# One core, a three-part matmul stream: longer first weight loads, a final norm by square root and reciprocal, and a store cut by tokens

## The chip, the cores and the metric

One core of a Trainium2 chip. The metric is the device time of one execution in microseconds; the number that counts is the median over runs.

## The reference

One decoder layer on x of shape (1, 256, 1024) in float32, then a final norm:

```
x = x + 0.5 * swiglu(rmsnorm(x, ffn1_norm), ...)           # D_FF = 2816
x = x + hybrid_mixer(rmsnorm(x, mix_norm), ...)            # S5 state space + attention, gated
x = x + 0.5 * swiglu(rmsnorm(x, ffn2_norm), ...)
return rmsnorm(x, final_norm)
# rmsnorm(x, g) = x * rsqrt(mean(x*x, over features) + 1e-6) * g
```

## The kernel before

x lies transposed in SBUF: 128 partitions by 8 feature tiles by 256 tokens. All weights come as one stream of units, each 128 partitions by 1024 float32 (512 KB, eight 128x128 tiles), in the order in which TensorE uses them. A unit n passes through three steps: `load(n, i)` fetches it on the SP queue into one of four staging buffers; `hi` copies it on ScalarE to a rounded 32-bit form (tile `wh`); `lo` subtracts that from the original on VectorE (tile `wl`). TensorE then makes three matmuls for each weight tile (L188 to L190): high weight by high x, high weight by low x, low weight by high x. x is split into `xh` and `xl` in the same way by `split_x`. A norm's factor is not applied to x ahead of a matmul but to the matmul's result.

The first stage is written out by hand (L872 to L895). Seven dummy matmuls (`warm_up`) run while the first data comes. Then the SP queue issues, in this order, x tile 0 with the gains, the first two quarters of unit 0, x tile 1, the second half of unit 0, x tiles 2 and 3, the halves of unit 1, x tiles 4 and 5, the halves of unit 2, x tiles 6 and 7, the halves of unit 3, and the identity. For each x tile k in turn, ScalarE and VectorE do the work of L888 to L894: split x tile k, split the piece or pieces of weights that belong to it, square x tile k for the norm. Each engine works in the order of the program. The first four outputs of the first feed-forward are computed together, so x tile k needs four weight tiles, half a unit: unit 0's first half for k = 0, its second half for k = 1, unit 1's first half for k = 2, and so on. From unit 4 on, units are loaded whole, each when a staging buffer comes free (`load_to`).

The second feed-forward ends with eight outputs m of its down projection. After each, `after_ffn2` squares x tile m and scales it by the final norm's gain. Then `norm(diag=False, ...)` sums the squares by matmuls into two columns (one for each half of the tokens, tile `nps`), and VectorE works out the inverse root on them with an integer trick and two polynomial steps (L245 to L253). Meanwhile TensorE transposes x back to tokens by features into four PSUM tiles `turned[i][h]` (token half i, feature half h). For each feature half h, ScalarE scales token half 0 and VectorE token half 1 into one tile, and the SP queue stores it with rows of 512 elements.

Of the kernel before, what the change touches and what calls it, by code (L numbers as in the profile page):

```python
# [10 lines left out]
F32 = mybir.dt.float32  # L11
F32R = mybir.dt.float32r
I32 = mybir.dt.int32
AF = mybir.ActivationFunctionType
ALU = mybir.AluOpType
# [4 lines left out]
D = 1024  # L20
# [8 lines left out]
UT = 8  # L29
# [7 lines left out]
RMS_EPS = 1e-6  # L37
# [24 lines left out]
def hybrid_layer(ctx: ExitStack, tc: tile.TileContext, xT, wst, consts, bc, out):  # L62
    nc = tc.nc
    V, S, G, PE = nc.vector, nc.scalar, nc.gpsimd, nc.tensor
    NU = wst.shape[0]

    cp = ctx.enter_context(tc.tile_pool(name="cp", bufs=1))
# [9 lines left out]
    def tt(out, a, b, op=ALU.mult, eng=None):  # L77
        (eng or V).tensor_tensor(out=out, in0=a, in1=b, op=op)  # L78

    def ts(out, a, s1, op0, s2=None, op1=None, eng=None):  # L80
        if op1 is None:
            (eng or V).tensor_scalar(out=out, in0=a, scalar1=s1, scalar2=None, op0=op0)
        else:
            (eng or V).tensor_scalar(out=out, in0=a, scalar1=s1, scalar2=s2, op0=op0, op1=op1)

    def stt(out, a, s, b, op0, op1):
        V.scalar_tensor_tensor(out=out, in0=a, scalar=s, in1=b, op0=op0, op1=op1)

    def act(out, a, func=AF.Copy, **kw):
        S.activation(out=out, in_=a, func=func, **kw)  # L90
# [11 lines left out]
    ones = cp.tile([128, 128], F32, name="ones")  # L102
    V.memset(ones, 1.0)
    warm = cp.tile([128, 1], F32, name="warm")
    act(warm, ones[:, 0:1], AF.Silu)
    halfpi = cp.tile([128, 1], F32, name="halfpi")
    V.memset(halfpi, math.pi / 2)
    inv = cp.tile([128, T], F32, name="inv")
    inv_tm = cp.tile([128, 2], F32, name="inv_tm")
    nrm = cp.tile([128, 2, 2], F32, name="nrm")  # L110
# [8 lines left out]
    staged, split = {}, {}  # L119
    state = {"load": 0, "hi": 0, "lo": 0, "at": -1, "hold": (3, 5)}  # L120
    LA = RB - 1

    def cuts(n):
        return [0, 256, 512, 1024] if n == 0 else [0, 512, 1024] if n <= 3 else [0, 1024]

    def load(n, i):
        if i == 0:
            staged[n] = stg.tile([128, UT * 128], F32, name="stage", tag="stage")
        c = slice(*cuts(n)[i:i + 2])
        nc.sync.dma_start(out=staged[n][:, c], in_=wst[n, :, c])  # L130

    def hi(n, i):
# [11 lines left out]

    def load_to(u):
        while state["load"] <= min(u, NU - 1):
            load(state["load"], 0)
            state["load"] += 1

    def split_hi(u):  # L150
        while state["hi"] <= min(u, NU - 1):
            load_to(state["hi"])
            hi(state["hi"], 0)
            state["hi"] += 1
# [11 lines left out]
    def ahead(u):  # L166
        split_hi(u + LA)
        split_lo(u + LA - 1)
        load_to(u + LA + 2)
        while deferred:  # L170
            deferred.pop(0)()
        if u in hooks:
            hooks.pop(u)()
# [47 lines left out]
    def square(k, first):  # L221
        add_squares()
        dst = acc if first else ev.tile([128, T], F32, name="sq", tag="sq")
        act(dst, x[:, k, :], AF.Square)
        if not first:
            squares.append(dst)

    def gram(t, y, v):
        for i in range(2):
            c = slice(i, i + 1)  # L230
            stt(t[:, c], y[:, c], y[:, c], v[:, c], ALU.mult, ALU.mult)

    def norm(pool=ps_a, tag="at", diag=True, between=None):
        ps = [pool.tile([128, 1], F32, name="nps", tag=tag) for _ in range(2)]
        terms = [acc] + squares
        squares.clear()
        for n, a in enumerate(terms):
            if between and n == len(terms) - 1:
                between()
            for i in range(2):  # L240
                for o in (0, 64):
                    PE.matmul(ps[i][o:o + 64, :], a[:, i * 128 + o:i * 128 + o + 64], ones[:, 0:1],
                              start=n == 0, stop=n == len(terms) - 1)
        v, t, y = nrm[:, 0, :], nrm[:, 1, :], inv_tm
        for i in range(2):  # L245
            ts(v[:, i:i + 1], ps[i], 1.0 / D, ALU.mult, RMS_EPS, ALU.add)
        ts(y.bitcast(I32), v.bitcast(I32), -0.5, ALU.mult, RSQRT_MAGIC, ALU.add)
        gram(t, y, v)
        stt(y, t, RSQRT_B, y, ALU.subtract, ALU.mult)
        gram(t, y, v)  # L250
        ts(v, t, -0.375 * RSQRT_A ** 5, ALU.mult, 1.25 * RSQRT_A ** 3, ALU.add)
        tt(v, v, t)
        stt(y, v, 1.875 * RSQRT_A, y, ALU.subtract, ALU.mult)  # L253
        if diag:
            diags.append(ev.tile([128, 2, 128], F32, name="dg", tag="sq"))
            for i in range(2):
                ts(diags[0][:, i, :], ident, y[:, i:i + 1], ALU.mult)
# [15 lines left out]
    def ffn(pool, bg, parts, norm_at, done, g):  # L273
        kh = KF // parts
        xh, xl = xv[g]
        for f in range(parts):
# [13 lines left out]
            for j in range(kh):  # L290
                if f == 0 and j < 2:
                    if j == 0:
                        first = [psum(i) for i in range(4)]
                        for k in range(KD):
                            for i in range(4):
                                mm3(first[i], pos[0], xh[:, k, :], xl[:, k, :], k == 0, k == KD - 1)
                                pos[0] += 1
                            if k == norm_at:
                                norm(ps_s, "s5")
                                if state["at"] in state["hold"]:  # L300
                                    ahead(state["at"])
# [566 lines left out]
    def load_x(k0, k1):  # L868
        c = slice(0 if k0 == 0 else 4 * KD + k0 * T, 4 * KD + k1 * T)
        nc.sync.dma_start(out=xg[:, c], in_=xT[:, c])  # L870

    warm_up(7)  # L872
    load_x(0, 1)
    load(0, 0)
    load(0, 1)
    load_x(1, 2)
    load(0, 2)
    load_x(2, 4)
    load(1, 0)
    load(1, 1)  # L880
    load_x(4, 6)
    load(2, 0)
    load(2, 1)
    load_x(6, 8)
    load(3, 0)
    load(3, 1)
    nc.sync.dma_start(out=ident, in_=consts[:, 0:128])
    for k, parts in ((0, ((0, 0), (0, 1))), (1, ((0, 2),)), (2, ((1, 0),)), (3, ((1, 1),)), (4, ((2, 0),)), (5, ((2, 1),)),  # L888
                     (6, ((3, 0),)), (7, ((3, 1),))):
# [32 lines left out]
    with tc.tile_pool(name="f2", bufs=1) as f2:  # L922
        last = f2.tile([128, T], F32, name="last")

        def after_ffn2(m):
            if m < KD - 1:
                square(m, m == 0)
            else:
                tt(last, x[:, m, :], x[:, m, :])
                squares.append(last)  # L930
            act(x[:, m, :], x[:, m, :], scale=gn[:, 3, m:m + 1])

        ffn(f2, idle, FH2, 4, after_ffn2, 2)
        turned = [[(ps_m if i == 0 else ps_s).tile([128, 512], F32, name="tps", tag="mm" if i == 0 else "s5")
                   for h in range(2)] for i in range(2)]

        def turn_x(m):
            for i in range(2):
                o = 128 * (m % 4)
                PE.transpose(turned[i][m // 4][:, o:o + 128], x[:, m, i * 128:(i + 1) * 128], ident)  # L940

        norm(diag=False, between=lambda: [turn_x(m) for m in range(4)])
        for m in range(4, KD):
            turn_x(m)
        for h in range(2):
            o = f2.tile([128, 2, 512], F32, name=f"out{h}")
            act(o[:, 0, :], turned[0][h], scale=inv_tm[:, 0:1])
            ts(o[:, 1, :], turned[1][h], inv_tm[:, 1:2], ALU.mult)
            nc.sync.dma_start(out=out.rearrange("(i p) d -> p i d", i=2)[:, :, 512 * h:512 * h + 512], in_=o)


def _perm():
# [109 lines left out]
```

## Time and profile before

| | us |
|---|---|
| median of 3 runs | 558.54 |
| lowest, highest | 558.08, 563.71 |
| the profiled execution, device time | 557.2 |
| its span, first to last instruction | 555.3 |
| TensorE busy within the span | 544.5 |
| VectorE busy | 399.2 |
| ScalarE busy | 309.1 |

The profile is one execution, taken apart by the hardware profiler. Times are from the span's start. TensorE's matmuls are pipelined: one of 256 columns is listed with 0.28 us, though the next one starts 0.11 us later. A DMA appears twice: as an instruction of the queue that issues it, and by its landing, the time from issue until all of it has arrived.

### The profile page before, as it was taken

Reading aid. Unit: us, or ns where it says so; the run is one execution under the profiler, and the core shown is the slowest. Engines: PE = TensorE matmul, PEld = TensorE weight load, DVE = VectorE, ACT = ScalarE, POOL = GpSimd, SP = SyncE. Lnnn points to the kernel's source line nnn. Section 1 sums busy time; section 2 is a strip of 40 time slices with the busy share of each in tenths; the row PEclk is TensorE's granted clock in tenths of the full one; section 3 lists DMA queues with packets and bytes.
Section 4 is the critical chain, followed back from the end, with each engine's and each line's share of the span. In section 5 each row is a group of like instructions: output and inputs, shape, how many; then the busy total and the mean of one; then the engine's idle time right before and its main releaser. Section 6 shows DMA issues by size and latency. Waiting matters only on the chain.

```text
span 555.3 us, 11894 instructions
## 1 busy us (share of the span) xinstructions
PE 544.5 (98%) x4860; PEld 534.5 (96%) x4860; DVE 399.2 (72%) x657; ACT 309.1 (56%) x477; POOL 80.3 (14%) x150
## 2 busy tenths in 40 slices
PE   7999999999999999999999999999999999999994
PEld 7999999999999989989999999999999999999994
DVE  5886798888865776999845888786766666665643
ACT  7764546559575683336547665565555444455421
POOL 0288951957000000000000000000000000000000
PEclk9999999999999999999999999999999999999998
DMA  8876666557564445265342656564755555666502
GB/s 281 297 253 195 193 194 216 156 157 229 175 201 159 145 152 152 77 208 191 105 145 77 203 185 186 187 209 164 228 195 192 191 190 193 194 210 204 173 15 77
DMA packets 28678, 99.30 MB, mean 179 GB/s; under 512 B 3152, under 2 KB 3792, under 8 KB 28624
## 3 DMA queue, kind: packets, MB, share of 16 engines
q1 hardware_dynamic: 28624, 98.54, 55.0%
q8 instruction: 38, 0.62, 0.4%
q14 instruction: 16, 0.13, 0.1%
HBM read 97.48 MB, written 1.05 MB: 177 GB/s over the span
## 4 chain that ended last, share of the span: by engine, by line
PE 94%; DVE 3%; DMA 1%; issue 1%; SPq 0%; DVEq 0%; ACT 0%
PE mm L188 20%; PE mm L189 19%; PE mm L190 19%; PE mma L188 8%; PE mma L189 8%; PE mma L190 8%; PE bps L615 1%; PE sps L714 1%; DMA stage<-in_wst_dram 1%; PE yps L662 1%; PE ops L744 1%; DVE wl L78 1%; PE up L584 1%; PE up L586 1%; PE vp L586 1%; PE vp L585 1%
## 5 line engine op out<-in xcount | busy, mean ns | idle before, releaser
L78 DVE TENSOR_TENSOR wl<-stage,wh 128x1024 fp32r<-128x1024 f32 (+2 forms) x187 | 223.3, 1201 | 15.0 <-ACT wh L90 14.8
L90 ACT ACTIVATE wh<-stage 128x1024 fp32r<-128x1024 f32 (+2 forms) x187 | 191.5, 1030 | 56.3 <-PE mm L189 26.3
L188 PE MATMUL mm<-xhl,wh 128*128 128x256 f32 x544 | 152.1, 280 | 2.2 <-ACT wh L90 2.2
L190 PE MATMUL mm<-xhl,wl 128*128 128x256 f32 x544 | 150.9, 277 | 0.4 <-DVE wl L78 0.4
L189 PE MATMUL mm<-xhl,wh 128*128 128x256 f32 x544 | 150.4, 277 | 0.0
L188 PEld LDWEIGHTS mm<-xhl,wh 128*128 128x128 f32 x544 | 102.1, 188 | 3.5 <-ACT wh L90 2.4
L190 PEld LDWEIGHTS mm<-xhl,wl 128*128 128x128 f32 x544 | 102.2, 188 | 1.0 <-DVE wl L78 0.8
L189 PEld LDWEIGHTS mm<-xhl,wh 128*128 128x128 f32 x544 | 102.2, 188 | 0.1
L188 PE MATMUL mma<-xhl,wh 128*128 128x256 f32 x352 | 97.7, 278 | 0.0
L188 PE MATMUL mm<-ahl,wh 128*128 128x256 f32 x352 | 97.5, 277 | 0.0
L190 PE MATMUL mm<-ahl,wl 128*128 128x256 f32 x352 | 97.2, 276 | 0.0
L189 PE MATMUL mm<-ahl,wh 128*128 128x256 f32 x352 | 97.2, 276 | 0.0
L189 PE MATMUL mma<-xhl,wh 128*128 128x256 f32 x352 | 97.2, 276 | 0.0
L190 PE MATMUL mma<-xhl,wl 128*128 128x256 f32 x352 | 97.2, 276 | 0.0
L188 PEld LDWEIGHTS mm<-ahl,wh 128*128 128x128 f32 x352 | 66.1, 188 | 0.2 <-issue 0.2
L188 PEld LDWEIGHTS mma<-xhl,wh 128*128 128x128 f32 x352 | 66.1, 188 | 0.1
L189 PEld LDWEIGHTS mma<-xhl,wh 128*128 128x128 f32 x352 | 66.1, 188 | 0.1
L190 PEld LDWEIGHTS mm<-ahl,wl 128*128 128x128 f32 x352 | 66.1, 188 | 0.0
L189 PEld LDWEIGHTS mm<-ahl,wh 128*128 128x128 f32 x352 | 66.1, 188 | 0.0
L190 PEld LDWEIGHTS mma<-xhl,wl 128*128 128x128 f32 x352 | 66.0, 188 | 0.0
L90 ACT ACTIVATE gs<-gs 128x256 f32<-128x256 f32 x52 | 21.8, 418 | 54.1 <-DVE gs L78 53.8
L78 DVE TENSOR_TENSOR gs<-gs,mma 128x256 f32<-128x256 f32 x44 | 18.5, 419 | 38.5 <-PE mma L190 33.7
(214 smaller groups left out, 730.8 us busy)
## 6 DMA issues: line engine op xcount, KB each, us to landing
stage<-in_wst_dram SPq DMA_DIRECT2D x178, 512.0 KB, 3.7
stage<-in_wst_dram SPq DMA_DIRECT2D x7, 256.0 KB, 5.5
out_dram<-out SPq DMA_DIRECT2D x2, 512.0 KB, 3.2
xg<-in_xT_dram SPq DMA_DIRECT2D x3, 256.0 KB, 5.8
bct<-in_bc_dram SPq DMA_DIRECT2D x1, 512.0 KB, 5.5
cst<-in_consts_dram SPq DMA_DIRECT2D x1, 396.0 KB, 4.7
stage<-in_wst_dram SPq DMA_DIRECT2D x2, 128.0 KB, 2.5
xg<-in_xT_dram SPq DMA_DIRECT2D x1, 144.0 KB, 2.1
```

The costliest lines, as they stand in the source:

```text
L78: (eng or V).tensor_tensor(out=out, in0=a, in1=b, op=op)
L90: S.activation(out=out, in_=a, func=func, **kw)
L188: PE.matmul(ps, wh, xh, start=start, stop=False)
L189: PE.matmul(ps, wh, xl, start=False, stop=False)
L190: PE.matmul(ps, wl, xh, start=False, stop=stop)
L584: PE.matmul(acc2[i], xh[:, k, sl], wh, start=k == 0, stop=False)
L585: PE.matmul(acc2[i], xh[:, k, sl], wl, start=False, stop=False)
L586: PE.matmul(acc2[i], xl[:, k, sl], wh, start=False, stop=k == KD - 1)
L615: PE.matmul(bp[part][o, gp, :], Rt[part][:, 8 * h + gp, o], Uc[:, 8 * h + gp, :], start=True, stop=True)
L662: PE.matmul(ypf[64 * par:64 * par + 64, gg, :], l, r.rearrange("p a b -> p (a b)"), start=term == 0, stop=term == 2)
L714: PE.matmul(sps[e][:, blk, :].rearrange("p a b -> p (a b)"), q[r, i, qs], k[r, i, ks], start=part == 0, stop=part == 1)
L744: PE.matmul(op[:, i, e, :], pq[:, b, :], v[:, j, h, :], start=j == 0, stop=b != 1)
```

## The change

Three parts. The first stage's loads of weights are fewer: unit 0 comes in two halves and not in two quarters and a half, units 1, 2 and 3 each whole and not in two halves. The pieces in which `hi` and `lo` split them stay as they were. The final norm takes a square root on ScalarE (`refine`), a reciprocal on VectorE, and one Newton step in place of the integer trick and two polynomial steps; a dummy square root after the first output of the last down projection brings its function table in. The output is gathered by token halves, a full row of 1024 elements each, the first stored from the SP queue, the second from ScalarE's.

```diff
+    eps = cp.tile([128, 1], F32, name="eps")
+    V.memset(eps, RMS_EPS)
...
-    def load(n, i):
-        if i == 0:
+    def load(n, *c):
+        if n not in staged:
             staged[n] = stg.tile([128, UT * 128], F32, name="stage", tag="stage")
-        c = slice(*cuts(n)[i:i + 2])
+        c = slice(*c)
         nc.sync.dma_start(out=staged[n][:, c], in_=wst[n, :, c])
...
+    def refine(ps, v, t, y):
+        for i in range(2):
+            act(y[:, i:i + 1], ps[i], AF.Sqrt, scale=1.0 / D, bias=eps)
+        V.reciprocal(out=y, in_=y)
+        tt(t, y, y)
+        tt(t, t, v)
+        ts(t, t, -0.5, ALU.mult, 1.5, ALU.add)
+        tt(y, y, t)
...
         for i in range(2):
             ts(v[:, i:i + 1], ps[i], 1.0 / D, ALU.mult, RMS_EPS, ALU.add)
+        if not diag:
+            return refine(ps, v, t, y)
...
     load_x(0, 1)
-    load(0, 0)
-    load(0, 1)
+    load(0, 0, 512)
     load_x(1, 2)
-    load(0, 2)
+    load(0, 512, 1024)
     load_x(2, 4)
-    load(1, 0)
-    load(1, 1)
+    load(1, 0, 1024)
     load_x(4, 6)
-    load(2, 0)
-    load(2, 1)
+    load(2, 0, 1024)
     load_x(6, 8)
-    load(3, 0)
-    load(3, 1)
+    load(3, 0, 1024)
...
         def after_ffn2(m):
+            if m == 0:
+                act(warm, ones[:, 0:1], AF.Sqrt)
...
-        for h in range(2):
-            o = f2.tile([128, 2, 512], F32, name=f"out{h}")
-            act(o[:, 0, :], turned[0][h], scale=inv_tm[:, 0:1])
-            ts(o[:, 1, :], turned[1][h], inv_tm[:, 1:2], ALU.mult)
-            nc.sync.dma_start(out=out.rearrange("(i p) d -> p i d", i=2)[:, :, 512 * h:512 * h + 512], in_=o)
+        for i in range(2):
+            o = f2.tile([128, D], F32, name=f"out{i}")
+            act(o[:, 0:512], turned[i][0], scale=inv_tm[:, i:i + 1])
+            ts(o[:, 512:D], turned[i][1], inv_tm[:, i:i + 1], ALU.mult)
+            (nc.sync, S)[i].dma_start(out=out[i * 128:(i + 1) * 128, :], in_=o)
```

## Rows read from the trace of the kernel before

**Rows 1.** The page, part 1: busy time of each engine, share, instructions

```profile
PE 544.5 (98%) x4860; PEld 534.5 (96%) x4860; DVE 399.2 (72%) x657; ACT 309.1 (56%) x477; POOL 80.3 (14%) x150
```

**Rows 2.** Waits of TensorE, whole span: total us, times, longest us

```profile
PE mm L188 <- ACT wh L90: 2.2, 1, 2.2
...
PE mm L190 <- DVE wl L78: 0.4, 2, 0.2
```

**Rows 3.** The chain that ended last, first 18 us: start, us, what

```profile
3.55 5.47 DMA stage<-in_wst_dram
...
17.06 0.35 DVE acc L78
```

**Rows 4.** Timeline of ScalarE, first stage: start, us, operation, idle before and releaser

```profile
4.28 0.42 ACT L90 ACTIVATE wh<-stage 128x256 fp32r<-128x256 f32 x1 [0.30 <-DMA stage<-in_wst_dram]
...
4.91 0.49 ACT L90 ACTIVATE xhl<-xg 128x256 fp32r<-128x256 f32 x1
7.48 0.63 ACT L90 ACTIVATE wh<-stage 128x512 fp32r<-128x512 f32 x1 [2.08 <-DMA stage<-in_wst_dram]
...
9.04 0.63 ACT L90 ACTIVATE wh<-stage 128x512 fp32r<-128x512 f32 x1 [0.16 <-DMA stage<-in_wst_dram]
...
11.56 0.62 ACT L90 ACTIVATE wh<-stage 128x512 fp32r<-128x512 f32 x1
```

**Rows 5.** Timeline of the SP queue, first stage: DMA issues

```profile
1.19 0.90 SPq L130 DMA_DIRECT2D stage<-in_wst_dram  x2
...
2.60 0.43 SPq L130 DMA_DIRECT2D stage<-in_wst_dram  x1
...
3.55 0.91 SPq L130 DMA_DIRECT2D stage<-in_wst_dram  x2
```

**Rows 6.** DMA issues at 1.19, 2.60 and 4.02 us: us to landing

```profile
stage<-in_wst_dram SPq DMA_DIRECT2D x1, 128.0 KB, 2.4
...
stage<-in_wst_dram SPq DMA_DIRECT2D x1, 256.0 KB, 4.9
...
stage<-in_wst_dram SPq DMA_DIRECT2D x1, 256.0 KB, 5.7
```

**Rows 7.** Windows: length, busy by engine, granted clock, DMA share, GB/s

```profile
0.00:3.00 3.00, 1.95 (x9) 1.95 (x10) 0.17 (x2) 1.61 (x3) 0.20 (x4) 1.00 0.31 93
3.00:6.00 3.00, 2.95 (x19) 2.61 (x18) 1.82 (x4) 1.92 (x5) 0.00 (x0) 1.00 0.86 281
9.00:12.00 3.00, 3.00 (x25) 2.91 (x26) 2.70 (x7) 2.96 (x7) 0.00 (x0) 1.00 1.07 399
551.00:553.90 2.90, 0.00 (x0) 0.00 (x0) 0.00 (x0) 0.00 (x0) 0.00 (x0) 0.50 0.97 362
```

**Rows 8.** Groups by line and shape: busy us, mean ns, idle before

```profile
L90 ACT ACT_TABLE_LOAD x5 | 6.4, 1283 | 0.8 <-PEq L1048 0.7
L90 ACT ACTIVATE sm<-sm,halfpi 128x16 f32<-128x16 f32 x1 | 0.3, 307 | 0.0
L746 DVE RECIPROCAL sme<-ops 128x4 f32<-128x4 f32 x4 | 0.7, 175 | 0.0
```

**Rows 9.** Timelines of ScalarE, TensorE, VectorE and SP, last down projection to the store

```profile
493.96 0.42 ACT L90 ACTIVATE acc<-xg 128x256 f32<-128x256 f32 x1 [1.96 <-DVE xg L78]
...
546.78 0.51 ACT L90 ACTIVATE xg<-xg 128x256 f32<-128x256 f32 x1 [6.98 <-DVE last L78]
...
547.21 1.09 PE L940 MATMUL tps<-cst,xg 128*128 128x128 f32 x8
...
547.21 0.27 DVE L84 TENSOR_SCALAR nrm<-nps 128x1 f32<-128x1 f32 x2 [0.47 <-PE nps L242]
...
549.08 0.16 DVE L87 SCALAR_TENSOR_TENSOR inv_tm<-nrm,inv_tm 128x2 f32<-128x2 f32 x1
549.28 1.41 DVE L82 TENSOR_SCALAR out<-tps,inv_tm 128x512 f32<-128x512 f32 x2
...
550.12 1.04 SPq L949 DMA_DIRECT2D out_dram<-out  x2
```

More of the change, by code (lines that the diff above doesn't have):

```diff
@@ L146, in load_to @@
         while state["load"] <= min(u, NU - 1):
-            load(state["load"], 0)
+            load(state["load"], 0, UT * 128)
             state["load"] += 1
```

## The prediction

> **What bounds the kernel now.** I began with the page's busy times: TensorE is busy 544.5 of 555.3 us [rows 1], so a gain can only come from the stretches in which it is not. The waits of TensorE say where those are [rows 2]: one wait of 2.2 us for ScalarE's copy of a weight (`wh`), 0.4 us for VectorE's `wl`, and nothing that repeats over the hundreds of microseconds between. So the middle of the kernel is left alone, and I read only the two ends.
>
> At the start, the chain of waits goes through a landing weight load from 3.55 to 9.02 us, then alternates between ScalarE and VectorE until the last `acc` addition at 17.06 [rows 3]; from there on it is TensorE. What comes earlier at 17.41 (17.06 + 0.35), where the norm's sums begin, comes earlier at the end, since no wait after it could swallow it [rows 2]. ScalarE's timeline shows the hole: it is done with x tile 1 at 5.40 (4.91 + 0.49) and starts on the second half of unit 0 at 7.48, after 2.08 us idle for that DMA [rows 4]. That load was issued at 2.60 and landed 4.9 us later [rows 5, 6].
>
> At the end, the last matmul sums reach VectorE at 547.21, two small instructions for v and eight behind them last until 549.28, then come the two scalings per engine, 1.41 us on VectorE, and two stores, the second issued near 550.75 (the two issues span 550.12 to 551.16, some 0.41 each) [rows 9]. The stores' bytes move from about 551.0 to 553.9 [rows 7].
>
> **The first loads.** Each DMA issue takes its place on the SP queue about 0.47 us after the one before (two in 0.90 us, 2.60 to 3.55 for two) [rows 5]. Merging the two quarters of unit 0 saves one issue ahead of everything else, so the second half of unit 0 is issued at 2.12 and not 2.60; unit 1 whole at 3.07 (its halves: 3.55 and 4.02), unit 2 at 4.02, unit 3 at 4.97.
>
> The bytes in the queue, though, decide more than the issue. Up to the end of unit 0 they are 144 + 128 + 128 + 128 + 256 = 784 KB (0.80 MB), before and after. By 3.0 us 0.28 MB had moved (93 GB/s over 3 us), then 281 GB/s [rows 7]. At that pace the 0.80 MB are through at 3 + 0.52/0.281 = 4.85. What lies between the last byte and the landing I take from the second quarter of unit 0: 0.41 MB are through at 3.46, ScalarE starts on it at 4.28 [rows 4], so 0.8 us. Unit 0 should then have landed near 5.65. It landed at 7.5. So 1.8 us of that landing is not explained by bytes or by issue; one slow piece of the transfer would do it, and no view names its cause. I treat it as an accident of this execution, with a chance of coming again.
>
> After the change, without it: unit 0's first half lands as one piece between 3.6 (where its first quarter landed, 1.19 + 2.4 [rows 5, 6]) and 4.28; I take 4.0, as one issue of 0.47 is gone from the second quarter's way. ScalarE then does two copies of 256 columns, the square and x tile 1, at the pace of 4.28 to 5.40 for three of them [rows 4] plus 0.36 for one more, and is free near 5.5; the second half of unit 0 lands near 5.65. ScalarE starts on it at about 5.6, which is 7.48 - 5.6 = 1.88 us earlier. TensorE's first matmul comes some 0.4 us later than before, at no cost: its twelve matmuls for x tile 0 still end before that.
>
> The Trainium skill, "DMA: Bandwidth & Descriptors", section Anatomy of one DMA, gives about 2.0 us plus the bytes at 436 GB/s for one DMA (fitted on another issuing engine): 2.3 us for 128 KB, where the row has 2.4 [rows 6]. By it the merged 256 KB would land at 1.19 + 2.6 = 3.8, an estimate that is 0.2 earlier than mine; the sum would not move, since ScalarE then waits for the second half instead.
>
> The 1.88 us holds only if units 1 and 2 keep up. ScalarE wants unit 1 at 9.04 - 1.88 = 7.16 and unit 2 at 11.56 - 1.88 = 9.68 [rows 4]. Bytes up to the end of unit 1 are 1.59 MB, to the end of unit 2 2.38 MB, by the order of issue. At 281 GB/s they land at 3 + 1.31/0.281 + 0.8 = 8.5 and 3 + 2.10/0.281 + 0.8 = 11.3; at the 399 GB/s that the queue reached from 9 to 12 us, at 7.1 and 9.1 [rows 7]. So the gain is between 0.3 (late by 1.6 for unit 2) and 1.88. Rows of 4 KB in place of 2 KB, no slow piece in between, and deeper queued work speak for the upper rate, the x tiles, whose rows stay short, for the lower. I take **-1.2 us**. From 9 to 17 us ScalarE and VectorE are full (VectorE 2.70 and ScalarE 2.96 of the 3 us from 9 to 12 [rows 7]), so the hole cannot shrink by more than its own length.
>
> **The dummy square root.** It brings a table load of 1.28 us [rows 8] and a one-column instruction (below 0.31 us, what 16 columns took [rows 8]) onto ScalarE just before the first square of the last down projection, where it stood idle for 1.96 us until 493.96 [rows 9]. Hidden: 0. Without that cover it would delay the weight copies by 1.6 us, which are made units ahead. The extra memset at the start is one small VectorE instruction while TensorE waits for data anyway: 0.
>
> **The final norm.** Removed: from 547.48 (547.21 + 0.27) to 549.28, eight VectorE instructions in a row, 1.8 us. Added: two square roots on ScalarE. It is free at 547.29 (546.78 + 0.51), just when the sums are there [rows 9]. The nearest row for one is 128x16 with a bias column, 307 ns [rows 8]; successive instructions on ScalarE start before the one ahead is listed as ended (4.91 follows an instruction at 4.61 of 0.40 [rows 4] by 0.30), so I take 0.30 + 0.21 and 0.05 for the hand-over to VectorE: 547.85. Then reciprocal, two products, one affine, one product: 0.19 each (549.08 to 549.28 is 0.20, a reciprocal lasts 0.175 [rows 8, 9]): 0.95. Scaling starts at 548.80, not 549.28: **-0.5 us**. Bounds: square roots of 0.15 each with no gap, -0.7; both at 0.31 plus 0.10 for the hand-over, -0.3. The two instructions for v run beside the square roots.
>
> **The store.** The second store of before was issued at 550.75, just after VectorE's second scaling ended at 550.69 (549.28 + 1.41) [rows 9]; the first issue had ended at 550.53. So the SP queue did not hold it up, and a second queue saves nothing. The halves of tokens change which transposed tiles come first; the last of these are ready at 548.30 (547.21 + 1.09 [rows 9]), before 548.80. Rows of 4 KB in place of 2 KB could lift the 362 GB/s of the store towards the 399 GB/s of loads [rows 7]: 1.05 MB in 2.63 rather than 2.9 us. I take **-0.1 us**, bounds +0.4 (a slower issue from ScalarE, which no row shows; one SP issue as its price) and -0.3.
>
> **Sum.** -1.2 - 0.5 - 0.1 = -1.8 us. Against its own device time, 557.2, that is 555.4. The median of the runs shown is 558.54, 1.3 above the profiled one, and may hold fewer or more slow pieces at the start; applied to it the same sum gives **556.7**.
>
> **The rivals.** *The slow piece comes again, or was not in the other runs.* Either way the start gains only about 0.3 to 0.5 against the median: in the first case unit 0 lands 4.9 us after 2.12, at 7.0, in place of 7.5. Sum -0.4 - 0.6 = -1.0: 557.5. For it: the landing is unexplained. Against: the loads of 128 KB beside it landed in 2.4 [rows 6].
>
> *The longer loads hold up whole units (the other side: slower).* Before, unit 1 could be split by halves; ScalarE started on the first at 9.04, while the second half, issued at 4.02 + 5.7, landed at 9.7 [rows 4 to 6]. If transfers flow as slowly as in this trace, the whole unit 1 is there at 8.5 by bytes and, with the slow piece of 1.8 on it, at 10.3: 1.3 late. Minus 0.6 at the tail, +0.7: 559.2. It decides from a landing of unit 1 after 9.04 + 0.6 = 9.64. Against: every byte of unit 1 is ahead of as many bytes as before, and is issued 0.5 to 1 us sooner.
>
> *The square root's table is lost again.* If a square or a copy between m = 0 and the tail needs another table, the load of 1.28 [rows 8] falls on the tail: -1.2 + 1.28 - 0.5 - 0.1 = -0.5: 558.0. Only five table loads in 555 us, with copies and squares beside several functions, speak against it [rows 8]. The Trainium skill, "ScalarE: Activation LUTs", section Table sets: the hidden batching unit, says copies are in every set but names no square in the square root's; no row here shows that pair. At the 2.66 us that the same page gives for a switch, the sum would be +0.9, 559.4 by estimate.
>
> *The square root gains nothing*, the hop between engines eating 0.5: 557.2.
>
> **How the numbers follow.** Forecast 0.50; slow piece 0.26; longer loads 0.12; table 0.06; no gain in the norm 0.06. The forecast's own range is 555.4 (-1.88 - 0.7 - 0.3 = -2.9 from 557.2 is 554.3, from 558.54 is 555.7) to 557.5. With the rivals, and own time and median both as starting points: 554.3 to 559.2. A change of 1% (5.6 us), which is about what a measurement of this kernel can tell from no change, is more than all terms together: the whole hole at the start and the whole norm are 2.1 + 1.8. One of three runs was 0.9% above the median, so a little is left to each side: faster 0.04, same 0.93, slower 0.03.
>
> **What would show it.** ScalarE's copy of unit 0's second half starts near 5.6, the norm's sums near 16.2 in place of 17.41; unit 1's landing before 7.2 shows the upper rate. One table load near 492, none after 545. Scaling starts 1.6 us after the sums reach VectorE, not 2.07. The stores' bytes end some 4.6 us after the scaling starts, as before, or 0.1 sooner. Wrong would make it: a wait of TensorE for unit 1 or 2 as long as the one that went, a table load in the tail, or a later second store.

## The result and the profile after

The change made the kernel slower: 560.71 us, the median of 22 runs (559.95 to 565.98), against 557.36 for the kernel before in 22 runs beside it. The ratio is 1.0057, with a 95% interval of 1.0034 to 1.0079. The forecast was 556.7 within 554.3 to 559.2. The time lies outside the range, and the kernel moved the other way.

The page of the profiled execution of the changed kernel (565.24 us of device time, a high one of its kind, see below) begins:

```profile
span 563.4 us, 11888 instructions
...
PE 554.0 (98%) x4860; PEld 543.5 (96%) x4860; DVE 398.4 (71%) x654; ACT 310.7 (55%) x481; POOL 76.4 (14%) x150
```

TensorE makes the same 4860 matmuls as in [rows 1], and is busy 9.5 us longer with them. Its waits have not grown in sum. The line between those of [rows 2] (waiter, what it waited for, total us, times, longest), and then the whole list of after:

```profile
PE wps L116 <- DVE halfpi L107: 1.0, 1, 1.0
```

```profile
PE wps L118 <- DVE eps L109: 1.0, 1, 1.0
PE mm L190 <- DVE gs L78: 0.7, 1, 0.7
PE mm L190 <- ACT wh L90: 0.6, 1, 0.6
PE mm L192 <- DVE wl L78: 0.4, 2, 0.2
```

The wait of 2.2 us of [rows 2] is down to 0.6; a new one of 0.7 us, for VectorE's tile `gs`, has come soon after the first norm; in all it is 2.7 us against 3.6. So the loss is not a wait, and the list of waits cannot show it. What shows it is a count of matmuls in windows of equal length. The columns are the window, its length, then busy us and, in brackets, instructions started on TensorE, its weight loader, VectorE, ScalarE and GpSimd, then granted clock, DMA share and GB/s. Before:

```profile
40.00:100.00 60.00, 60.00 (x532) 60.00 (x531) 45.61 (x66) 31.95 (x42) 37.29 (x88) 1.00 0.61 194
320.00:350.00 30.00, 30.00 (x267) 30.00 (x267) 23.52 (x39) 16.77 (x27) 0.00 (x0) 1.00 0.62 195
420.00:520.00 100.00, 100.00 (x885) 100.00 (x884) 62.11 (x86) 50.31 (x70) 0.00 (x0) 1.00 0.59 193
```

After:

```profile
40.00:100.00 60.00, 60.00 (x512) 60.00 (x511) 43.37 (x62) 29.84 (x40) 31.29 (x87) 1.00 0.61 197
320.00:350.00 30.00, 30.00 (x257) 30.00 (x256) 23.62 (x40) 15.30 (x24) 0.00 (x0) 1.00 0.62 198
420.00:520.00 100.00, 100.00 (x884) 100.00 (x884) 62.23 (x88) 52.11 (x74) 0.00 (x0) 1.00 0.61 196
```

The reader is to see that TensorE is listed as 100% busy in all six windows, at a granted clock of 1.00, and that it nevertheless started 512 matmuls where it had started 532, and 257 where it had started 267. From start to start that is 113 ns before and 117 ns after, on the mean of the window; the expectations, which go by single starts, say 118. In the last window, the second feed-forward, the pace is the same. The stretches at the slower pace are the first part of the first feed-forward (about 18 to 132 us) and the second half of the mixer: attention gate, GLU, branches and output projection (about 300 to 372 us). Parts of the stretch between lose a little too: 1528 matmuls started from 132 to 300 us, where it was 1535. The change touches no line of any of these.

One cut makes the comparison of runs easy: the start up to the norm's first sums, the middle from there to the last norm's first sums, and the tail behind those. The cuts are the first and the last start of `nps<-ones,acc` on TensorE's timeline, and the end is the span's:

| kernel | start | middle | tail | profiled time | median |
|---|---|---|---|---|---|
| before | 17.45 | 527.84 | 10.0 | 557.2 | 557.36 |
| after | 17.44 | 536.66 | 9.3 | 565.24 | 560.71 |
| after, a second profile | 18.14 | 537.46 | 9.6 | 566.99 | |
| eps tile alone | 16.89 | 531.40 | 10.0 | 560.21 | 560.80 |
| whole change, eps in the unused tile | 17.70 | 528.04 | 9.4 | 556.90 | 556.83 |
| first loads alone | 17.78 | 527.83 | 10.0 | 557.45 | 557.72 |
| whole change but the first loads, eps in the unused tile | 17.09 | 528.02 | 9.5 | 556.33 | 556.34 |

The new tail gains 0.4 to 0.7 us in every kernel that has it. The new start gains nothing. The middle loses 3.6 us where only the eps tile was added, and 8.8 us in the profile of the changed kernel, which holds an extra 5 us in the first feed-forward (the wait of 0.7 us for `gs` is in it). That part comes and goes between executions: of the 22 runs of the changed kernel 3 lie above 565 and 16 below 561.2. The kernel before has runs as far above its median too: 3 of its 22 lie between 561.5 and 563.7, but none of those was profiled.

### The profile page after: what moved, and what is told of

Read it like the earlier page. It is cut to its first block, busy times and chain, and to the rows that moved or that the text cites. A ratio compares the mean times of both kernels' runs of the same rounds, so it can differ in the third digit from the quotient of the medians.

```text
span 563.4 us, 11888 instructions
## 1 busy us (share of the span) xinstructions
PE 554.0 (98%) x4860; PEld 543.5 (96%) x4860; DVE 398.4 (71%) x654; ACT 310.7 (55%) x481; POOL 76.4 (14%) x150
## 4 chain that ended last, share of the span: by engine, by line
PE 92%; DVE 3%; ACT 2%; DMA 1%; issue 1%; SPq 0%; DVEq 0%
PE mm L190 20%; PE mm L192 19%; PE mm L191 19%; PE mma L190 8%; PE mma L191 8%; PE mma L192 8%; PE bps L628 1%; PE sps L727 1%; DMA stage<-in_wst_dram 1%; PE yps L675 1%; ACT wh L90 1%; PE ops L757 1%; DVE wl L78 1%; PE up L597 1%; PE vp L599 1%; PE vp L598 1%
```

## The experiments

The expectations set three theories against each other: A, the place of the operands in SBUF sets TensorE's pace; B, the new first loads leave TensorE in another rhythm; C, the square root's table load or its wait disturbs ScalarE.

**Is it the new tile's place?** The changed kernel allocates a tile `eps` in the middle of the first pool. It takes 32 bytes of each partition and moves every tile behind it up by as much: the norm's tiles, the tile of x's high and low parts (from byte 31200 to 31232), the ring of split weights (47840 to 47872) and all later pools. These places come from the allocator, not from the trace. The first run adds only that tile to the kernel before.

```diff
     V.memset(halfpi, math.pi / 2)
+    eps = cp.tile([128, 1], F32, name="eps")
+    V.memset(eps, RMS_EPS)
```

> The kernel before with nothing but the eps tile and its memset, which moves every SBUF tile allocated behind it (inv, acc, xhl, the rings, ahl) up by 32 bytes; eps is not used. Theory A (the place of the operands in SBUF sets the pace of the matmuls, 113 or 118 ns from start to start): slower than before by 3 to 4 us, with stretches at 118 ns in the second feed-forward's gate and up matmuls, as in the changed kernel. Theory B (the different first loads leave TensorE in another rhythm, and addresses do not matter): same as before within 0.5 us, and 113 ns there. Theory C (the square root's table load or its new wait disturbs ScalarE): same as before.

Measured: 560.80 us (6 runs, 560.21 to 564.85), 1.0067 of before (1.0041 to 1.0092). That is the whole loss, with a tile that nothing reads. Its windows:

```profile
40.00:100.00 60.00, 60.00 (x531) 60.00 (x531) 45.59 (x67) 31.43 (x41) 37.28 (x89) 1.00 0.62 198
320.00:350.00 30.00, 30.00 (x257) 30.00 (x257) 22.85 (x38) 16.01 (x24) 0.00 (x0) 1.00 0.59 181
420.00:520.00 100.00, 100.00 (x885) 100.00 (x884) 61.16 (x86) 49.41 (x70) 0.00 (x0) 1.00 0.61 196
```

The mixer runs at 257 matmuls, as in the changed kernel. The first feed-forward runs at 531, as before. So the mixer's loss belongs to the tile, and the other one did not occur in this execution. The expectation called the slow stretch the second feed-forward's gate and up matmuls. That was a misreading: the operands listed from 320 to 350 us (xhl, zh, zl, mh) are the mixer's, and the second feed-forward, behind 372, keeps its pace. The later expectations that speak of the second feed-forward carry the same misreading.

The second run is the whole change, with eps in a column of a tile that both kernels allocate and never use.

```diff
-    ev.tile([128, 16], F32, name="shift", bufs=1)
+    shift = ev.tile([128, 16], F32, name="shift", bufs=1)
...
-    eps = cp.tile([128, 1], F32, name="eps")
+    eps = shift[:, 0:1]
     V.memset(eps, RMS_EPS)
```

> The whole change, but eps lies in a column of the tile named shift, which is allocated and unused in both kernels, so that every other tile has the address it had before. Theory A: the 3 us of loss are gone, and what is left is the gain of the tail and of the start, 0.4 to 1.5 us faster than before. Theory B and theory C: slower than before by about 3 us, as the change itself.

Measured: 556.83 us (12 runs, 556.21 to 558.85), 0.9997 of before (0.9984 to 1.0010). With every tile back at its address, the loss is gone and the middle is 528.04 again. (By the allocator, two of the five buffers of `wl`, 8192 bytes apart, change places wherever units are loaded whole; the run with the first loads alone has that as well, and a middle of 527.83.) Theories B and C fall. But no gain is left that can be told from no change.

**What do the first loads and the rest do by themselves?** The third run has the loads alone, the fourth everything but the loads (eps in the unused tile).

```diff
     load_x(0, 1)
-    load(0, 0)
-    load(0, 1)
+    load(0, 0, 512)
...
-    load(1, 0)
-    load(1, 1)
+    load(1, 0, 1024)
```

> The kernel before with only the fewer and longer first loads. Theory A: within 0.5 us of before, since the norm's sums began at the same 17.4 us in both profiles. Theory B: slower by about 3 us, with the 118 ns stretches. Theory C: same as before.

Measured: 557.72 us (12 runs), 1.0009 of before (0.9998 to 1.0021). No gain, and if anything a small loss.

```diff
     load_x(0, 1)
-    load(0, 0, 512)
+    load(0, 0)
+    load(0, 1)
...
-    load(1, 0, 1024)
+    load(1, 0)
+    load(1, 1)
```

> The change without its first loads (they are as before), with eps in the unused tile so that no address moves: the new norm, the dummy square root and the stores by token halves. Theory A: 0.3 to 0.6 us faster than before, the shorter norm alone. Theory B: the same 0.3 to 0.6 us faster. Theory C: slower by about 3 us.

Measured: 556.34 us (12 runs), 0.9980 of before (0.9956 to 1.0004), a gain of 0.9 us between the medians, though the interval reaches past 1. Theory C is out for good: with the square root and its table load in it, the middle is 528.02.

**Which part of the loads costs?** Only unit 0's quarters merged; units 1 to 3 by halves again, the rest of the change with eps in the unused tile.

```diff
-    load(1, 0, 1024)
+    load(1, 0, 512)
+    load(1, 512, 1024)
...
-    load(3, 0, 1024)
+    load(3, 0, 512)
+    load(3, 512, 1024)
```

> The change with eps in the unused tile, but units 1, 2 and 3 loaded by halves as before; only unit 0's first two quarters are merged. If the whole-unit loads are what costs the half microsecond that separates the run with all of the change (556.8) from the one without its loads (556.3): 556.0 to 556.4. If the merged first load is what costs it: 556.8. If the loads make no difference and that half microsecond is scatter: anything between.

Measured: 556.49 us (10 runs, 555.70 to 556.99), 0.9980 of before (0.9960 to 1.0000), with a start of 16.96. The median lies just outside the 556.0 to 556.4 that the whole-unit loads would give, nearer to it than to 556.8. So it is likely the whole-unit loads, but the times alone do not show it: the four profiles with them start the norm at 17.44 to 18.14, this one and that of the run without the new loads at 16.96 and 17.09. Other kernels with the old loads scatter from 16.3 to 17.9, so this is a shift of half a microsecond in a scatter of one, carried by the medians (556.83 against 556.34 and 556.49) rather than by any single profile.

**Does the second queue do anything?** Norm and store as in the run without the new loads, both stores from the SP queue.

```diff
-            (nc.sync, S)[i].dma_start(out=out[i * 128:(i + 1) * 128, :], in_=o)
+            nc.sync.dma_start(out=out[i * 128:(i + 1) * 128, :], in_=o)
```

> The new norm and the store by token halves with first loads as before, both stores issued from the SP queue. If the second queue saves nothing: the stretch from the first scaling to the end stays at 5.8 us, and the time at 556.3. If the second queue is the source of the 0.24 us that this stretch gained: it is back at 6.06 us, the time at 556.6.

Measured: 556.22 us (10 runs), 0.9989 of before (0.9961 to 1.0017). From the first scaling (550.07) to the end (555.9) it takes 5.8 us, as with two queues (548.73 to 554.6), against 6.0 before. The second queue saves nothing that one profile each can show; the 0.2 us come with the store's new shape.

**Whose place is it?** Two runs move x and the weights against each other. The first puts x's two parts 32 bytes further inside their tile and moves nothing else; the second puts an unused tile of 32 bytes behind x's.

```diff
-X_AT = (48, 48, 48)
+X_AT = (56, 56, 56)
```

> The kernel before with x's high and low parts placed 32 bytes further inside their tile (offset 56 in place of 48 elements) and nothing else moved; the work is the same. Theory A1 (the place of the moving operand x sets the pace): the 118 ns stretches of the run with eps alone, 560.5 to 561. Theory A2 (the place of the weights in the ring, or of something else behind x): same as before, 557.3, at 113 ns. Theory A3 (the distance between x and the weights counts): slow here and slow where the rest is moved.

```diff
     xhl = cp.tile([128, 2 * KD * T + SLACK], F32R, name="xhl")
+    cp.tile([128, 8], F32, name="pad")
```

> The kernel before with an unused tile of 32 bytes put behind x's: x, inv and acc stay, the weights' ring, the staging buffers and all later tiles move up by 32 bytes. Theory A1: same as before, 557.3. Theory A2: 560.5 to 561 with the 118 ns stretches. Theory A3: slow, as where x alone is moved.

Measured: 570.56 us (4 runs), 1.0226 of before (1.0177 to 1.0276), and 569.47 us (4 runs), 1.0208 (1.0150 to 1.0266). Either move costs 12.5 to 13.5 us, some three and a half times what moving both together costs. The windows of the run with x moved:

```profile
40.00:100.00 60.00, 60.00 (x511) 60.00 (x510) 43.83 (x62) 30.50 (x41) 31.39 (x85) 1.00 0.63 198
320.00:350.00 30.00, 30.00 (x260) 30.00 (x259) 24.66 (x43) 16.62 (x24) 0.00 (x0) 1.00 0.67 203
420.00:520.00 100.00, 100.00 (x855) 100.00 (x854) 60.41 (x85) 48.79 (x69) 0.00 (x0) 1.00 0.59 191
```

Now the second feed-forward slows as well, from 885 to 855 matmuls. The distance between x and what lies behind it matters most (theory A3). But it is not all, or the run with eps alone, which keeps this distance, would not have been slow: the absolute place counts too, or the distance to the tiles in front of eps, which stayed.

Nor do a matmul's own operands settle its pace. The first down projection of the first feed-forward multiplies `ahl` by weights, and neither moved in this run. Its matmuls in 20 us (window, length, busy us and count of TensorE, clock, DMA share, GB/s), before and with x moved:

```profile
75.00:95.00 20.00, 20.00 (x179) 1.00 0.60 196
75.00:95.00 20.00, 20.00 (x172) 1.00 0.54 172
```

The slow pace reached them too, while the same projection in the second feed-forward kept the fast one (267 and 268 matmuls from 505 to 535 us). The first feed-forward is also the stage in which executions of one kernel differ (see below), so this need not come from the move; no run shows what carried the pace over.

**Does the pace repeat?** Three runs move everything behind eps together, by 64, 128 and 1024 bytes.

```diff
+    eps = cp.tile([128, 1], F32, name="eps")
+    V.memset(eps, RMS_EPS)
+    cp.tile([128, 8], F32, name="pad")
```

The unused tile has 8 columns here, 24 and 248 in the other two.

> The kernel before with the eps tile and an unused tile of 32 bytes beside it, so that inv and every tile behind it moves up by 64 bytes in place of 32; nothing else. If the pace goes by the place within 64 bytes, with the distance between x and the weights as before: same as before, 557.0 to 557.4, at 113 ns in the second feed-forward. If any move away from the tuned places costs: slower by 3 us or more, like the move by 32.

> The kernel before with the eps tile and an unused one behind it, so that inv and every later tile moves up by 128 bytes; nothing else. If the pace of the second feed-forward's gate and up matmuls repeats every 128 bytes when all tiles move together: 557 to 558 with 113 ns there. If it does not: 560 to 562 with 118 ns, as with 32 and 64.

> The same with 1024 bytes, the length of one x tile's row. If the pace repeats with the length of that row (or a part of it): 557 to 558 with 113 ns. If what counts is that the tiles lie where they were: 560 to 562 with 118 ns.

Measured: 561.04 us for 64 bytes (4 runs), 1.0057 of before (1.0035 to 1.0079); 563.15 for 128 (2 runs), 1.0111 (1.0034 to 1.0189); 557.64 for 1024 (8 runs), 0.9999 (0.9971 to 1.0027). The windows with 1024 bytes:

```profile
40.00:100.00 60.00, 60.00 (x532) 60.00 (x531) 45.66 (x66) 31.83 (x42) 37.12 (x86) 1.00 0.61 196
320.00:350.00 30.00, 30.00 (x267) 30.00 (x266) 23.44 (x40) 16.85 (x26) 0.00 (x0) 1.00 0.62 191
420.00:520.00 100.00, 100.00 (x885) 100.00 (x884) 61.67 (x86) 50.30 (x70) 0.00 (x0) 1.00 0.61 192
```

These are the counts of before, 532, 267 and 885. So it is not the new tile or its memset that costs, since they are here too, but where the others land. Of the moves tried only 1024 bytes brings the pace back; 256 and 512 were not tried, nor any multiple.

**The changed kernel once more**, as it is, for a second profile.

> The changed kernel itself once more, for a second profile. If the 118 ns from 18 to 132 us in its first profile belongs to single executions and the 118 ns of the second feed-forward to the kernel: a time near 560.6, 113 ns in the first feed-forward and 118 ns in the gate and up matmuls of the second. If both belong to the kernel: 565, 118 ns in both.

Measured: 566.99 us, with the slow pace in the mixer (257 matmuls from 320 to 350 us) and in the first feed-forward as well (512 from 40 to 100 us). So the changed kernel shows the slow first feed-forward in two profiles out of two, but in 3 to 4 of 22 runs by time: 16 of the 22 lie between 559.9 and 561.2, which has room for the mixer's 3.6 us and not for five more. The profiles with 64 and 128 bytes show it as well (512 each). Of the five profiled executions with all tiles moved together by 32 to 128 bytes, four show it; of the 30 other runs of these kernels, three are as far up (564.85 to 565.98). A profiled execution may fall into it more easily; no run tests that. One profile without the new loads and at the old addresses (both stores from SP) has a short piece of it, from 17 to 23 us, which ends at a wait of 1.0 us for `gs`. So this part is not shown to belong to the tile, and what decides in an execution whether the first feed-forward falls into the slow pace stays open.

## Why the prediction was wrong

**The step that failed** is in the prediction's first paragraph and in the last sentence on the dummy square root: "So the middle of the kernel is left alone", and "The extra memset at the start is one small VectorE instruction while TensorE waits for data anyway: 0." Both costed the eps tile by the instruction that fills it. Its price was the place it takes: 3.6 us in the middle. That is the 531.40 against 527.84 of the run with nothing but the tile, and the difference of the medians of the changed kernel with the tile and with eps elsewhere, 560.71 - 556.83 = 3.9. No rival named it, since all of them were sought among waits, queues and transfers. None of the listed signs of being wrong came either: no long wait for unit 1 or 2, no table load in the tail, no later second store. The kernel before bore a sign that could have been read: a tile `shift` that nothing uses (L71), and offsets of x and of the activations inside padded tiles (`SLACK`, `X_AT`, `A_AT`, L33 to L35). They compute nothing; all they do is set places. That they were chosen for the pace is not on record.

**The first loads** were the second error, in the largest of the terms that were worked out: forecast -1.2 us, measured about +0.5. The first half of the step was right. ScalarE's timeline after the change:

```profile
4.02 0.72 ACT L90 ACTIVATE wh<-stage 128x256 fp32r<-128x256 f32 x2 [0.55 <-DMA stage<-in_wst_dram]
...
6.31 0.63 ACT L90 ACTIVATE wh<-stage 128x512 fp32r<-128x512 f32 x1 [0.87 <-DMA stage<-in_wst_dram]
6.85 0.40 ACT L90 ACTIVATE sq<-xg 128x256 f32<-128x256 f32 x1
7.73 0.51 ACT L90 ACTIVATE xhl<-xg 128x256 fp32r<-128x256 f32 x1 [0.48 <-DMA xg<-in_xT_dram]
9.03 0.63 ACT L90 ACTIVATE wh<-stage 128x512 fp32r<-128x512 f32 x1 [0.79 <-DMA stage<-in_wst_dram]
```

Unit 0's first half starts at 4.02 (forecast 4.0), its second half at 6.31 in place of 7.48 [rows 4]: 1.2 us earlier, where 1.9 was hoped for. Then the gain is given back. x tiles 2 and 3 hold ScalarE until 7.73, and unit 1, which must now arrive whole, until 9.03, the very moment at which its first half was taken up before (9.04). From there on both kernels run alike to 17.4. The upper rate, on which the gain rested, did not come in time:

```profile
3.00:6.00 3.00, 2.92 (x14) 2.62 (x14) 1.73 (x4) 1.89 (x5) 0.00 (x0) 1.00 0.81 229
6.00:9.00 3.00, 2.88 (x19) 2.62 (x18) 1.18 (x2) 1.45 (x3) 0.00 (x0) 1.00 0.99 358
```

From 3 to 6 us the queue moved 229 GB/s, less than the 281 of before [rows 7], and only then more. In the nine profiles with the old loads that window has 233 to 289, in the four with the new ones 229 to 243. These ranges meet, so it is not shown that longer loads as such start more slowly. What the profiles do show is when ScalarE takes up unit 1: with the old loads, by its first half, at 7.50 to 9.17, in the middle at 8.68; with the new ones, whole, at 9.03 to 9.73; with unit 0 alone merged, by its first half again, at 8.55. Whole, it came later than the 7.1 to 8.5 at which the prediction let it land, at either rate. The rival of the longer loads was the right one in kind; its price, 1.3 us, was too high.

The unexplained 1.8 us of unit 0's landing was taken for an accident of one execution. That was half right. In the nine profiles with the old loads ScalarE took up that half at 5.88 to 7.48, in the middle at 6.44: later than the 5.65 worked out from bytes in every one, by 0.2 to 1.8. So the bytes' pace is not a bound on one load among several that are under way. But the profile that the prediction read has the latest of the nine. About 1 us of the hole of 2.08 belonged to that execution, and in a usual one there was less to gain. The first rival, that the other runs lacked the slow piece, was to that extent right.

**The norm** was right in kind and a little short. VectorE's timeline after:

```profile
556.02 0.27 DVE L84 TENSOR_SCALAR nrm<-nps 128x1 f32<-128x1 f32 x2 [0.47 <-PE nps L253]
556.66 0.17 DVE L238 RECIPROCAL inv_tm<-inv_tm 128x2 f32<-128x2 f32 x1 [0.36 <-ACT inv_tm L90]
...
557.45 0.16 DVE L78 TENSOR_TENSOR inv_tm<-inv_tm,nrm 128x2 f32<-128x2 f32 x1
557.72 1.41 DVE L82 TENSOR_SCALAR out<-tps,inv_tm 128x512 f32<-128x512 f32 x2
```

From the sums to the scaling it takes 1.70 us against 2.07 [rows 9], so -0.37 where -0.5 was forecast. The five VectorE instructions keep their 0.2 us each; what was missed is 0.1 us from the last of them to the scaling. The square roots (ScalarE's timeline) and the table load:

```profile
500.83 1.28 ACT L90 ACT_TABLE_LOAD   x1
502.12 0.20 ACT L90 ACTIVATE warm<-ones 128x1 f32<-128x1 f32 x1
502.77 0.42 ACT L90 ACTIVATE acc<-xg 128x256 f32<-128x256 f32 x1 [0.45 <-DVE xg L78]
...
556.21 0.41 ACT L90 ACTIVATE inv_tm<-nps,eps 128x1 f32<-128x1 f32 x2
```

The table load sits in the idle time before the first square, with 0.45 us to spare, and there is none in the tail. Squares and copies ran behind it without a reload: the rival of the lost table is out.

**The store** was right: -0.2 us where -0.1 was forecast, nothing from the second queue. Norm and store together are the 0.4 to 0.7 us of the tail in the table, against a forecast of 0.6.

**The sum of a usual run** then closes: +0.5 for the loads, -0.6 for the tail, +3.6 for the place make +3.5, against 560.71 - 557.36 = +3.35. The terms of the two ends are within a scatter of half a microsecond, so the agreement is partly luck. The forecast time also started too high: from 558.54, the median of three runs, where 22 runs give 557.36. From there its sum of -1.8 would have been 555.6, and the miss is 5.1 us and not 4.0: about 3.6 for the place and 1.7 for the loads, with nothing from the tail.

**A better version.** Without the new loads, or with unit 0 alone merged, and eps in the unused tile, the change gives 556.2 to 556.5 us. That beats the changed kernel by more than 4 us and the kernel before by 0.1 to 0.2%, with intervals that just reach 1.

## What to carry to other kernels

A new tile is priced by what it moves, not by what fills it. Where matmuls follow each other at a fixed pace, put a new constant into a column that is already allocated, or move the rest by an amount that is known to bring the pace back. When TensorE is listed as busy all the time, count its instructions in windows of equal length before and after: a list of waits does not show a pace that went from 113 to 117 ns. Merging loads that feed a pipeline by halves gives up the half that came first: here unit 1 was taken up some 0.7 us later. And a hole in one profile is worth a look at a second profile before its whole length is counted as a gain.

## What the runs showed of the hardware

In these runs TensorE's pace depends on where its operands lie. Moving x by 32 bytes against the ring of weights took the whole kernel from 557 to 570 us, moving both together by 32, 64 or 128 bytes to 561 to 563, and by 1024 bytes changed nothing. The pace holds for stretches of 60 us and more. In the first feed-forward it is not a matter of the operands' addresses alone: the changed kernel was profiled slow there twice and yet most of its runs are some 5 us shorter, and with x moved it was slow on `ahl` and weights that had not moved. Which accesses meet there was not tried: a run that moves the weights' ring without the later tiles, or x's high and low parts against each other, would narrow it.

The Trainium skill, "SBUF — State Buffer", section Who interferes with whom, gives TensorE two independent read ports, one for the operand that streams and one for the weights, and names a port pair that VectorE and GpSimd share as the only place where engines contend. By that alone the place of an operand would change nothing. Here, with the same instructions on all engines, 32 bytes between x and the weights cost 2%. The measurement decides, and the page's picture is not the whole of it; which ports or banks are behind the cost no run shows.
